# The decayed scores of a chunked recurrence: levels of 32 and 64 tokens as full 128 by 128 products with masks

## The chip, the core and the metric

The program runs on one core of one Trainium2 chip. Five engines work side by side, each through its own queue in the order of the program: TensorE (PE, with its weight loads shown apart as PEld), VectorE (DVE), ScalarE (ACT), GpSimd (POOL) and SyncE (SP, which issues the loads of weights). The metric is the device time of one execution in microseconds (us).

## What is computed

Two blocks of a language model run over 256 tokens of width 1024, in float32. The first block has two layers, and each has a mixer with a gated recurrence over 8 heads. That recurrence is what the change touches. It goes in chunks of 64 tokens, `gc` is the logarithm of the forget gate, and a state is carried from chunk to chunk:

```python
def step(state, inp):
    qc, kc, vc, gc = inp
    cum = jnp.cumsum(gc, axis=2)
    diff = cum[:, :, :, None, :] - cum[:, :, None, :, :]
    decay = jnp.where(causal, jnp.exp(jnp.where(causal, diff, 0.0)), 0.0)
    scores = jnp.einsum('bhtk,bhtsk,bhsk->bhts', qc, decay, kc)
    o = (jnp.einsum('bhts,bhsv->bhtv', scores, vc)
         + jnp.einsum('bhtk,bhkv->bhtv', qc * jnp.exp(cum), state))
...
```

Around it stand nine projections of the 256 tokens (values, forget gate, queries, a short convolution's three inputs, three gates), three output projections and a feed-forward; then come the mixture of experts and the second block. None of that is changed.

## The kernel before

Weights are streamed: SP loads pieces of 128 by 1024, ACT rounds each to a high part (`wh`, line 139), DVE subtracts to get the low part (`wl`, line 141), and PE does three products for each pair of tiles (lines 207 to 209: high by high, high by low, low by high). This is the main stream, written by `mixer` for the recurrence's part of the program. Six pieces of each part are held, so the splits run ahead of PE until that ring is full. A projection of 256 columns takes two pieces and 48 main products of 128 by 256.

The recurrence, `hgrn`, is a side generator. After half a projection and again after a projection, the main stream steps it twice (`tick`), at a lower priority; from these priorities a scheduler fixes each engine's order when the kernel is built. `hgrn` takes the eight heads in two halves of four, so the two layers together have four halves. A half computes the scores of every pair (s, t) in a tile of 128 tokens by levels. A first level (`md`) covers pairs within a block of 8. Then, for a block size m of 8, 16, 32, 64 and 128, the pairs with s in the left and t in the right half of a block of 2m are done: `e` holds keys decayed to the left half's end and queries decayed from there, and a product of `e` with itself gives their scores. For each level there are two steps of ACT and DVE work (lines 735 to 746) before its products.

What happens at each level before the change, for each of the two token tiles and four heads of a half:

- m = 8: one full 128 by 128 product per head into a PSUM bank, all four heads in one bank; then `put` copies the valid pairs to `Sc` by a mask on DVE (`copy_predicated`, line 724).
- m = 16: the same full products into a bank `hold` for each token tile, which is kept.
- m = 32: for each head two products of 32 by 32, written into corners of the bank of m = 16, over what stood there (lines 763 to 769).
- m = 64: for each head one product of 64 by 64, likewise; then one `put` per bank moves the levels 16, 32 and 64 together, by the mask `m16`.
- m = 128: one full product per head across the two token tiles.

All of these products go through `mm` (line 203); in the trace a float32 product stands as two matmul records with two weight loads. The side work has three PSUM banks (`sd`), of which `hold` keeps two from m = 16 to m = 64. At the end of a half, once the output gate `sg` is there, the scores meet the values, a norm is taken, and PE transposes the result (line 805), after which the last output projection but one can read it.

Of the kernel before, what the change touches and what calls it, by code (L numbers as in the profile page):

```python
# [16 lines left out]
P = 128  # L17
D = 1024
S = 256
NT = S // P  # L20
# [3 lines left out]
NE = 8  # L24
EPS = 1e-6
BIG = 1.0e30
# [21 lines left out]
class Kernel:  # L48
# [48 lines left out]
    # raws: what one DMA loads; pieces: what is split at a time into two parts of 12 bits each  # L97
# [11 lines left out]
    def pump(self, limit=1 << 30):  # L109
        nc = self.nc  # L110
        while True:
# [3 lines left out]
            i = self.dma_i  # L115
# [13 lines left out]
            if i < len(self.pieces) and i < self.freed + SPLIT_BUFS and self.pieces[i][0] < self.dma_i:  # L129
# [5 lines left out]
                with self.tc.high_priority(offset=SPLIT_SOONER):  # L135
                    # small operations where a phase's chain runs beside them
                    m = n // (FINE_BY if i in self.fine else 1)
                    for c in range(0, n, m):
                        nc.scalar.copy(hi[:, c:c + m], raw[:, c:c + m])  # L139
                        with self.tc.issue_after(self.hold) if self.hold is not None else nullcontext():  # L140
                            nc.vector.tensor_sub(lo[:, c:c + m], raw[:, c:c + m], hi[:, c:c + m].bitcast(F32))  # L141
# [10 lines left out]
    # while arenas are free, raws of the next phase go there  # L152
# [24 lines left out]
    # steps: how many of its steps follow each unit of the main stream  # L177
# [19 lines left out]
    def urgent(self):  # L197
        # no sooner than the last branch
        return self.tc.high_priority(offset=min(CHAIN_SOONER, self.tc.tile_snap_priority() - self.floor))

# [17 lines left out]
    def rsqrt_mean(self, ss, n):  # L218
        """(ss / n + eps) ** -0.5; overwrites ss"""
# [5 lines left out]
    def mean_sq(self, halves, c=1.0):  # L225
        """(c * c * mean of squares + c * c * eps) ** -0.5 over two halves of 512; c a power of two.
        halves: yields each half when it is there"""
# [19 lines left out]
    def prenorm(self, t, gt, out=None):  # L247
        """x[t] -> normalised tokens [128, 1024]"""
# [12 lines left out]
    def put_hT(self, t, xs):  # L261
        """transpose normalised tokens into hT hi/lo"""
# [15 lines left out]
    # boundary: post(t) puts the phase's output for token tile t into x  # L278
# [7 lines left out]
    # the second token tile's transposes come after the first tile's products  # L286
# [6 lines left out]
    def down(self, key, lhs, nk, post, to_next):  # L293
        """tokens-stationary product with K = nk*128, 1024 columns.
        post(t, banks): adds to x.  to_next: (prenorm, after T0 matmuls ...)"""
# [38 lines left out]
    def norm_next(self, gt):  # L334
        """steps to go from x to hT of the next phase, used by down()"""
# [18 lines left out]
    def norm_post(self, pg, scale):  # L354
        """x += scale * rmsnorm(product) * pg"""
# [12 lines left out]
    # weights-stationary projection: out [128, 2, 256]  # L368
# [20 lines left out]
    # tokens-stationary projection: out [128 tok, n, 256]  # L389
# [21 lines left out]
    def ffn(self, n, post, to_next):  # L411
# [4 lines left out]
        def finish_g(g, gt):  # L416
            """gt: [128 tok] x T tiles of G columns"""
# [63 lines left out]
    def consts(self):  # L481
        nc = self.nc
        g = nc.gpsimd
        # small per-channel parameters: rows in, columns out
# [26 lines left out]
        # lower bounds: cumulated softmax over the two layers, less its first  # L511
# [19 lines left out]
        # masks over [s, t]  # L531
# [4 lines left out]
        v16 = lambda t: t.rearrange("p (n i) -> p n i", i=16)  # L536
        self.m16 = self.cst("m16", [P, P])      # t in a later block of 16 than s
        g.memset(self.m16, 1.0)
        sel(v16(self.m16), [[16, 8], [0, 16]], -1, -1)
        self.m8 = self.cst("m8", [P, P])        # same block of 16, t in its second half, s in its first  # L540
        g.memset(self.m8, 1.0)
        sel(v16(self.m8), [[16, 8], [0, 16]], 15, -1)
        sel(v8(self.m8), [[8, 16], [0, 8]], -1, -1)
        self.md = self.cst("md", [P, P])        # same block of 8, s <= t
# [30 lines left out]
    def mixer(self, l, post, to_next):  # L575
# [13 lines left out]
        # forget gate  # L589
# [20 lines left out]
        # short convolution of b * u, gated by c  # L610
# [71 lines left out]
    def hgrn(self, l, V, LF, Kt, Qt, box):  # L682
        """decayed scores by halving: for block sizes m the pairs (s in a left half, t in the
        right half) are referred to the left half's end, so no exponent is above 0; inside
        blocks of 8 the middle is the reference and exponents stay within 8 * ln(1e-6) / 2"""
        nc = self.nc
        mul, sub, add = nc.vector.tensor_mul, nc.vector.tensor_sub, nc.vector.tensor_add
        # scores are kept 2**-20 smaller, so that no product overflows outside the blocks either
# [5 lines left out]
        for h in range(2):  # L694
# [38 lines left out]
            hold = None  # L733
            for m in (8, 16, 32, 64, 128):
# [13 lines left out]
                if m == 8:  # L748
                    for t in range(NT):
# [4 lines left out]
                        put(t, pt, self.m8)  # L754
                        yield
                elif m == 16:
                    hold = [self.sd_ps((P, 4, P)) for _ in range(NT)]
                    for t in range(NT):
                        for j in range(4):
                            c = slice(j * S + t * P, j * S + (t + 1) * P)  # L760
                            self.mm(hold[t][:, j, :], e[:, c], e[:, c], True, True)
                    yield
                elif m in (32, 64):
                    for t in range(NT):
                        for j in range(4):
                            for b in range(0, P, 2 * m):
                                c = j * S + t * P + b
                                self.mm(hold[t][b:b + m, j, b + m:b + 2 * m], e[:, c:c + m],
                                        e[:, c + m:c + 2 * m], True, True)
                    if m == 64:  # L770
                        for t in range(NT):
                            put(t, hold[t], self.m16)
                    yield
# [7 lines left out]
            # values, norm over a head's values, output gate  # L781
# [58 lines left out]
    def moe_consts(self):  # L840
# [6 lines left out]
        self.tri = t[:, 2, :]                   # s < t  # L847
# [6 lines left out]
        self.jlt = t[:, 4, 0:NE * NE].rearrange("p (e j) -> p e j", j=NE)  # j < e  # L854
# [7 lines left out]
        # the norm's gain goes with the features, its factor with the tokens  # L862
        nc.vector.tensor_mul(self.rw, self.rw, bc(self.moe_g.unsqueeze(2), [P, KD, NE]))

    def moe_enter(self):
        """from x to tokens in two parts, and each token's place with its experts; the norm's
        factor does not change the order of the logits and is put to the experts' products"""
# [39 lines left out]
    def route(self, t, pl):  # L907
        """the two experts of each token"""
# [3 lines left out]
        # rank of each expert: greater logits, or equal ones at a lower index, come first  # L912
# [10 lines left out]
    def places(self):  # L923
        """place of each token in its expert's list, and the places' one-hot"""
# [12 lines left out]
    def gates(self):  # L937
        """softmax over the chosen two; the largest count of an expert's tokens"""
# [20 lines left out]
    def moe_places(self):  # L959
        """one-hot with the places on the partitions"""  # L960
# [9 lines left out]
    def gather(self, q):  # L970
        """the tokens of experts 2q, 2q + 1, features on the partitions"""
# [19 lines left out]
    def slots_r(self, ohs, out):  # L991
        """the norm's factor of the token at each place"""
# [96 lines left out]
    def final_norm(self, nxt):  # L1089
        """x[t] = rmsnorm(x[t]) * fin, and the next phase's norm of that"""  # L1090
# [5 lines left out]
        def after(t):  # L1096
# [13 lines left out]
            # mean square of w * r without a further pass  # L1110
# [18 lines left out]
    def moe_rest(self):  # L1129
        """experts with more than 128 tokens: their places 128..255"""  # L1130
# [99 lines left out]
    def consts2(self):  # L1230
        """relative bias, causal masks, window counts, head masks"""
        nc, g, I = self.nc, self.nc.gpsimd, self.ins
        c = self.arena(7, (P, 16, P))
        self.R = c[:, 0:8, :].rearrange("p (h a) b -> p h (a b)", h=4)       # bias of (t, s), t in the second tile
        self.invc = c[:, 8, 0:16]
        self.cpen = c[:, 12, :]                 # 0 where s <= t, else -BIG  [t, s]
# [3 lines left out]
        self.ki4 = c[:, 13, :]                  # row c to rows 32 h + c  # L1240
# [4 lines left out]
        self.hm = c[:, 14, 0:8]                 # four 32-row heads, two 64-row heads  # L1245
# [7 lines left out]
        # 1 / (t + 1)  # L1253
        g.iota(self.invc, pattern=[[1, 16]], base=1, channel_multiplier=0, allow_small_or_imprecise_dtypes=True)
        nc.vector.reciprocal(self.invc, self.invc)
        # bias by distance, then one row per t through DRAM
# [4 lines left out]
        n1 = 255                                # rv[j] = bias of distance max(255 - j, 0)  # L1261
# [7 lines left out]
        # row t reads rv[127 - t : 127 - t + 256]; loaded with t reversed, turned by a permutation  # L1269
# [25 lines left out]
    def mix2_params(self, l):  # L1295
        """tiles and parameters of the mixing; their arenas are free once the feed-forward before is
        past its first 8 row blocks of w_down"""
# [27 lines left out]
    def mix2(self, l, post, to_next):  # L1325
# [9 lines left out]
        # token-layout values of gmlp and attention  # L1335
# [8 lines left out]
        # index queries, keys and weights  # L1344
# [423 lines left out]
```

## Time and profile before

| | us |
|---|---|
| three runs | 2904.30, 2908.52, 2911.13 |
| their median | 2908.52 |
| span of the profiled execution | 2903.8 |
| PE busy in it | 2846.2 |
| PEld busy | 2575.5 |
| DVE busy | 2023.8 |
| ACT busy | 1643.3 |
| POOL busy | 84.6 |

The span runs from the first to the last instruction of the program in the profiled execution; the timed runs include what lies around it. PE's records overlap, since products are pipelined, so a busy PE can still be a slow one: what a product costs is read from the distance between the starts of neighbours in the timeline, not from its record's length. The granted clock of a stretch is 1.00 at 2.4 GHz and 0.50 at 1.2 GHz.

### The profile page before, as it was taken

The page shows a single profiled execution, that of the slowest core. Times are in us where ns is not written, and L with a number is a line of the kernel's source. Part 1 is how long each engine was busy: PE and PEld are TensorE (multiplying, and loading weights), DVE is VectorE, ACT ScalarE, POOL GpSimd, SP SyncE. Part 2 cuts the span into 40 slices and gives each one's busy share as a digit, 9 for nine tenths or more (in the row PEclk, how much of TensorE's full clock was granted, in tenths as well). Part 3 has the DMA queues.
Part 4 walks back from the last instruction along what each step waited for, and adds up shares of the span by engine and source line. Part 5 has one row for each costly group of instructions (what it writes and reads, how often), then busy time and mean ns, then how long its engine had stood idle before and what let it go on. Part 6 is the DMA issues. An engine that isn't in the chain of part 4 may idle for free. (4 is left out here: it accounts for less than half of the span.)

```text
span 2903.8 us, 47599 instructions
## 1 busy us (share of the span) xinstructions
PE 2846.2 (98%) x18752; PEld 2575.5 (89%) x18752; DVE 2023.8 (70%) x2631; ACT 1643.3 (57%) x2188; POOL 84.6 (3%) x161
## 2 busy tenths in 40 slices
PE   8999999999999999999999989999999999999999
PEld 8998999999898887877877779899999899899997
DVE  5665655576659888888888865579765555697654
ACT  6543544564447776777777754466554444565543
POOL 1000000000000000000000010100000001000000
PEclk9998999999999999999999989999999999999999
DMA  7453565555456999999999965654655556546553
GB/s 248 145 175 102 177 192 186 186 160 158 155 190 223 331 333 350 338 341 353 329 345 359 346 209 185 198 170 135 204 189 186 187 186 200 168 137 199 183 182 109
DMA packets 425047, 635.00 MB, mean 219 GB/s; under 512 B 20186, under 2 KB 298896, under 8 KB 424816
## 3 DMA queue, kind: packets, MB, share of 16 engines
q1 hardware_dynamic: 421184, 621.65, 65.1%
q0 software_dynamic: 3632, 10.24, 1.3%
q8 instruction: 148, 2.42, 0.4%
q14 instruction: 83, 0.68, 0.1%
HBM read 630.76 MB, written 1.05 MB: 218 GB/s over the span
## 5 line engine op out<-in xcount | busy, mean ns | idle before, releaser
L141 DVE TENSOR_TENSOR wl<-wr,wh 128x1024 fp32r<-128x1024 f32 (+2 forms) x1265 | 1408.9, 1139 | 605.4 <-ACT wh L139 596.4
L139 ACT CAST wh<-wr 128x1024 fp32r<-128x1024 f32 (+2 forms) x1265 | 1201.0, 983 | 709.9 <-PE mm L208 360.9
L207 PE MATMUL mm<-hhi,wh 128*128 128x256 f32 x3360 | 961.8, 286 | 0.0
L208 PE MATMUL mm<-hlo,wh 128*128 128x256 f32 x3360 | 959.7, 286 | 0.0
L209 PE MATMUL mm<-hhi,wl 128*128 128x256 f32 x3360 | 958.7, 285 | 0.0
L207 PEld LDWEIGHTS mm<-hhi,wh 128*128 128x128 f32 x3360 | 646.1, 192 | 3.2 <-issue 2.0
L208 PEld LDWEIGHTS mm<-hlo,wh 128*128 128x128 f32 x3360 | 646.3, 192 | 1.9 <-issue 0.7
L209 PEld LDWEIGHTS mm<-hhi,wl 128*128 128x128 f32 x3360 | 646.2, 192 | 1.4 <-issue 0.3
L208 PE MATMUL mm<-wl,a 128*128 128x512 f32 (+1 forms) x1336 | 514.1, 385 | 2.2
L207 PE MATMUL mm<-wh,a 128*128 128x512 f32 (+1 forms) x1336 | 509.9, 382 | 0.0
L209 PE MATMUL mm<-wh,a 128*128 128x512 f32 (+1 forms) x1336 | 508.3, 380 | 0.0
L208 PEld LDWEIGHTS mm<-wl,a 128*128 128x128 f32 x1336 | 251.3, 188 | 65.9 <-DVE wl L141 17.5
L207 PEld LDWEIGHTS mm<-wh,a 128*128 128x128 f32 x1336 | 251.4, 188 | 49.6 <-issue 1.5
L209 PEld LDWEIGHTS mm<-wh,a 128*128 128x128 f32 x1336 | 251.5, 188 | 45.5
L208 PE MATMUL sd<-wl,a 128*128 128x512 f32 x352 | 145.2, 412 | 1.1
L209 PE MATMUL sd<-wh,a 128*128 128x512 f32 x352 | 140.1, 398 | 3.7 <-PEq L1132 3.7
L207 PE MATMUL sd<-wh,a 128*128 128x512 f32 x352 | 117.4, 399 | 0.0
L207 PE MATMUL mm<-a,wh 128*128 128x256 f32 x384 | 113.8, 296 | 0.0
L208 PE MATMUL mm<-a,wh 128*128 128x256 f32 x384 | 113.0, 294 | 0.0
L209 PE MATMUL mm<-a,wl 128*128 128x256 f32 x384 | 112.7, 294 | 0.0
L212 ACT CAST a<-t 128x256 fp32r<-128x256 f32 (+1 forms) x114 | 49.3, 432 | 108.9 <-DVE t L453 105.8
L209 PE MATMUL mm<-wh,hlo 128*128 128x256 f32 x352 | 104.5, 297 | 2.8 <-DVE hlo L213 2.8
(323 smaller groups left out, 2528.7 us busy)
## 6 DMA issues: line engine op xcount, KB each, us to landing
wr<-in_expert_w_dram SPq DMA_DIRECT2D x515, 512.0 KB, 5.4
wr<-in_w_in_dram SPq DMA_DIRECT2D x240, 512.0 KB, 3.9
wr<-in_ffn_w_gu_dram SPq DMA_DIRECT2D x176, 512.0 KB, 3.5
wr<-in_ffn_w_down_dram SPq DMA_DIRECT2D x88, 512.0 KB, 3.4
wr<-in_dense_w_dram SPq DMA_DIRECT2D x66, 512.0 KB, 3.6
wr<-in_w_out_dram SPq DMA_DIRECT2D x32, 512.0 KB, 4.1
wr<-in_w_proj_conv_dram SPq DMA_DIRECT2D x16, 512.0 KB, 4.5
wr<-in_w_proj_hgrn_dram SPq DMA_DIRECT2D x16, 512.0 KB, 4.5
```

The source lines that it names most:

```text
L139: nc.scalar.copy(hi[:, c:c + m], raw[:, c:c + m])
L141: nc.vector.tensor_sub(lo[:, c:c + m], raw[:, c:c + m], hi[:, c:c + m].bitcast(F32))
L207: mm(out, l[0], r[0], start=start, stop=False)
L208: mm(out, l[0], r[1], start=False, stop=False)
L209: mm(out, l[1], r[0], start=False, stop=stop)
L212: self.nc.scalar.copy(hi, src)
```

## The change

Levels 8, 16, 32 and 64 all do the same full product of `e` with itself per head and token tile, into a bank of their own that is freed at once. What a full product yields outside the level's own pairs is wrong, and later levels overwrite it: the mask of a level takes every pair in which t lies in a later block of m than s, and the greater levels come after. For m = 64 the valid part is one rectangle, so ACT copies it without a mask. `hold` is gone. Levels 16, 32 and 64 each have a step per token tile now, so a half has three steps more. The masks are `m8`, `m16` and `m32` by one rule; one `affine_select` fewer is done at the start. All other lines of the diff are comments.

```diff
-        self.m16 = self.cst("m16", [P, P])      # t in a later block of 16 than s
-        g.memset(self.m16, 1.0)
-        sel(v16(self.m16), [[16, 8], [0, 16]], -1, -1)
-        self.m8 = self.cst("m8", [P, P])        # same block of 16, t in its second half, s in its first
...
+        self.later_block = {}
+        for m in (8, 16, 32):
+            t = self.later_block[m] = self.cst(f"m{m}", [P, P])
+            g.memset(t, 1.0)
+            sel(t.rearrange("p (n i) -> p n i", i=m), [[m, P // m], [0, m]], -1, -1)
...
-            hold = None
             for m in (8, 16, 32, 64, 128):
...
-                if m == 8:
+                if m < 128:
                     for t in range(NT):
                         pt = self.sd_ps((P, 4, P))
                         for j in range(4):
                             c = slice(j * S + t * P, j * S + (t + 1) * P)
                             self.mm(pt[:, j, :], e[:, c], e[:, c], True, True)
-                        put(t, pt, self.m8)
+                        if m == 64:
+                            nc.scalar.copy(Sc[0:64, 2 * t, :, 64:P], pt[0:64, :, 64:P])
+                        else:
+                            put(t, pt, self.later_block[m])
                         yield
-                elif m == 16:
-                    hold = [self.sd_ps((P, 4, P)) for _ in range(NT)]
-                    for t in range(NT):
-                        for j in range(4):
-                            c = slice(j * S + t * P, j * S + (t + 1) * P)
-                            self.mm(hold[t][:, j, :], e[:, c], e[:, c], True, True)
-                    yield
-                elif m in (32, 64):
-                    for t in range(NT):
-                        for j in range(4):
-                            for b in range(0, P, 2 * m):
-                                c = j * S + t * P + b
-                                self.mm(hold[t][b:b + m, j, b + m:b + 2 * m], e[:, c:c + m],
-                                        e[:, c + m:c + 2 * m], True, True)
-                    if m == 64:
-                        for t in range(NT):
-                            put(t, hold[t], self.m16)
-                    yield
```

PE, level of 32 tokens of the first half in the first layer. Before (`sd_` is a score bank, `t_` is `e`, `mm_` the main stream's bank):

```order
L203 MATMUL sd_1266<-t_169_1276 32x32
L207 MATMUL mm_1419<-hhi_145,wh_1209 128x256
L203 MATMUL sd_1266<-t_169_1276 32x32
L208 MATMUL mm_1419<-hlo_146,wh_1209 128x256
L203 MATMUL sd_1266<-t_169_1276 32x32
L209 MATMUL mm_1419<-hhi_145,wl_1210 128x256
L203 MATMUL sd_1266<-t_169_1276 32x32
L207 MATMUL mm_1419<-hhi_145,wh_1227 128x256
L203 MATMUL sd_1266<-t_169_1276 32x32
```

and in the changed kernel:

```order
L203 MATMUL sd_1349<-t_175_1317 128x128
L207 MATMUL mm_1405<-hhi_145,wh_1211 128x256
L203 MATMUL sd_1355<-t_175_1317 128x128
L203 MATMUL sd_1349<-t_175_1317 128x128
L208 MATMUL mm_1405<-hlo_146,wh_1211 128x256
L203 MATMUL sd_1355<-t_175_1317 128x128
L203 MATMUL sd_1349<-t_175_1317 128x128
L209 MATMUL mm_1405<-hhi_145,wl_1212 128x256
L203 MATMUL sd_1355<-t_175_1317 128x128
L203 MATMUL sd_1349<-t_175_1317 128x128
L203 MATMUL sd_1355<-t_175_1317 128x128
```

Of the sixteen narrow products, each of which had a main product behind it, none is left; eight full ones stand there, with three main products among them.

DVE, in the same half at the level of 64 tokens. Before (line 724 is `put`, 141 a weight split, 622 and 634 the convolution's work, 713 the next half's first step):

```order
L713 TENSOR_TENSOR t_298_2325<-a_41_184 128x1024
L141 TENSOR_TENSOR wl_1465<-wr_1150,wh_1464 128x1024
L622 TENSOR_TENSOR a_135_1000<-a_135_1000,mm_1419 128x2x256
L141 TENSOR_TENSOR wl_1483<-wr_1213,wh_1482 128x1024
L724 COPY_PREDICATED Sc_1029<-m_333,sd_1266 128x512
L724 COPY_PREDICATED Sc_1029<-m_333,sd_1267 128x512
```

and in the changed kernel (lines 722, 141, 620 and 632 are the same in its numbering; 741 is the last part of `e` for m = 128):

```order
L741 TENSOR_TENSOR t_195_1479<-t_195_1479,a_42_185 128x4x128
L632 SCALAR_TENSOR_TENSOR t_220_1678<-a_135_1002,cols,t_220_1678 128x256 x2
L722 COPY_PREDICATED Sc_1031<-m_339,sd_1349 128x512
L141 TENSOR_TENSOR wl_1455<-wr_1152,wh_1454 128x1024
L722 COPY_PREDICATED Sc_1031<-m_339,sd_1355 128x512
L620 TENSOR_TENSOR a_135_1002<-a_135_1002,mm_1405 128x2x256
```

Before, one pair of puts (`m_333` is `m16` there) closed the levels 16 to 64; now the levels 16 and 32 have a pair each (`m_339` is the mask of 32 tokens), with a weight split between its two.

## Rows read from the trace of the kernel before

**Rows 1.** The page's part 1, busy time by engine, and its clock line
```profile
PE 2846.2 (98%) x18752; PEld 2575.5 (89%) x18752; DVE 2023.8 (70%) x2631; ACT 1643.3 (57%) x2188; POOL 84.6 (3%) x161
...
PEclk9998999999999999999999989999999999999999
```

**Rows 2.** The page's part 4, the chain that ended last
```profile
PE 39%; DVE 2%; issue 1%; POOL 1%; ACT 0%; POOLq 0%; DVEq 0%; ACTq 0%
```

**Rows 3.** Waits of PE, in total, times, longest
```profile
PE sd L268 <- DVE t L254: 18.9, 13, 12.3
PE sd L805 <- DVE t L801: 9.2, 8, 2.3
PE sd L268 <- DVE t L1120: 8.6, 2, 6.5
```

**Rows 4.** Timeline of PE in a full level: start, us, line, tiles, count
```profile
118.22 0.38 PE L203 MATMUL sd<-t 128*128 128x128 f32 x2
118.36 0.37 PE L207 MATMUL mm<-hhi,wh 128*128 128x256 f32 x1
118.56 0.38 PE L203 MATMUL sd<-t 128*128 128x128 f32 x2
118.70 0.37 PE L208 MATMUL mm<-hlo,wh 128*128 128x256 f32 x1
...
120.51 0.38 PE L203 MATMUL sd<-t 128*128 128x128 f32 x2
120.65 0.36 PE L207 MATMUL mm<-hhi,wh 128*128 128x256 f32 x1
120.85 0.28 PE L208 MATMUL mm<-hlo,wh 128*128 128x256 f32 x1
120.97 0.28 PE L209 MATMUL mm<-hhi,wl 128*128 128x256 f32 x1
```

**Rows 5.** The same in a level of 32 tokens
```profile
123.46 0.25 PE L203 MATMUL sd<-t 128*32 128x32 f32 x2
123.64 0.39 PE L208 MATMUL mm<-hlo,wh 128*128 128x256 f32 x1
123.95 0.25 PE L203 MATMUL sd<-t 128*32 128x32 f32 x2
124.13 0.38 PE L209 MATMUL mm<-hhi,wl 128*128 128x256 f32 x1
124.44 0.25 PE L203 MATMUL sd<-t 128*32 128x32 f32 x2
```

**Rows 6.** The same in a level of 64 tokens
```profile
138.05 0.33 PE L203 MATMUL sd<-t 128*64 128x64 f32 x2
138.31 0.39 PE L208 MATMUL mm<-hlo,wh 128*128 128x256 f32 x1
138.63 0.33 PE L203 MATMUL sd<-t 128*64 128x64 f32 x2
138.88 0.38 PE L209 MATMUL mm<-hhi,wl 128*128 128x256 f32 x1
139.20 0.27 PE L203 MATMUL sd<-t 128*64 128x64 f32 x1
```

**Rows 7.** Four stretches: busy us (count) by engine, granted clock, DMA share, GB/s
```profile
core 0: us, PE busy (x) PEld busy (x) DVE busy (x) ACT busy (x) POOL busy (x), PEclk, DMA share, GB/s
122.97:143.89 20.92, 20.92 (x121) 16.40 (x121) 11.26 (x20) 4.63 (x6) 0.00 (x0) 0.84 0.30 98
248.22:272.52 24.30, 24.30 (x122) 18.32 (x122) 7.74 (x9) 5.02 (x5) 0.00 (x0) 0.65 0.19 64
643.91:666.04 22.13, 22.13 (x121) 17.11 (x121) 11.26 (x20) 4.63 (x6) 0.00 (x0) 0.77 0.29 93
769.69:789.97 20.28, 20.28 (x122) 15.55 (x121) 7.76 (x9) 5.04 (x5) 0.00 (x0) 0.83 0.38 127
```

**Rows 8.** The first of these stretches, line 203 alone: PE, PEld, clock
```profile
122.97:143.89 20.92, 6.81 (x48) 3.97 (x49) 0.84 0.30 98
```

**Rows 9.** Timeline of PE in a stretch at half clock
```profile
133.19 0.41 PE L209 MATMUL mm<-hhi,wl 128*128 128x256 f32 x1
133.40 0.41 PE L207 MATMUL mm<-hhi,wh 128*128 128x256 f32 x1
```

**Rows 10.** Weight loads of score products by shape: busy us, mean ns
```profile
L203 PEld LDWEIGHTS sd<-t 128*128 128x128 f32 x160 | 23.7, 191 | 0.0
L203 PEld LDWEIGHTS sd<-t 128*32 128x32 f32 x128 | 9.5, 119 | 10.1 <-issue 4.9
L203 PEld LDWEIGHTS sd<-t 128*64 128x64 f32 x64 | 7.0, 155 | 5.0 <-issue 2.0
```

**Rows 11.** The recurrence's first half in the first layer, busy us by engine
```profile
103.17:169.30 66.13, 66.13 (x503) 61.48 (x502) 51.26 (x76) 28.36 (x34) 0.00 (x0) 0.95 0.43 136
```

**Rows 12.** Groups of DVE, and of ACT, from 100 to 170 us: busy, mean ns, idle
```profile
L724 DVE COPY_PREDICATED Sc<-m,sd 128x512 f32<-128x512 int32 x4 | 2.9, 737 | 2.4 <-PE sd L203 2.4
L779 ACT COPY Sc<-sd 128x512 f32<-128x512 f32 x1 | 0.6, 578 | 0.0
```

**Rows 13.** Who waited for whom, in the whole span: total us, times, longest
```profile
DVE Sc L724 <- PE sd L203: 29.1, 14, 3.7
```

More of the change, by code (lines that the diff above doesn't have):

```diff
@@ L416, in finish_g @@
         def finish_g(g, gt):
+            pass
         gts = []
@@ L535, in consts @@
         v8 = lambda t: t.rearrange("p (n i) -> p n i", i=8)
-        v16 = lambda t: t.rearrange("p (n i) -> p n i", i=16)
-        self.m16 = self.cst("m16", [P, P])
-        g.memset(self.m16, 1.0)
-        sel(v16(self.m16), [[16, 8], [0, 16]], -1, -1)
-        self.m8 = self.cst("m8", [P, P])
-        g.memset(self.m8, 1.0)
-        sel(v16(self.m8), [[16, 8], [0, 16]], 15, -1)
-        sel(v8(self.m8), [[8, 16], [0, 8]], -1, -1)
+        self.later_block = {}
[3 more added lines that the diff above has]
+            sel(t.rearrange("p (n i) -> p n i", i=m), [[m, P // m], [0, m]], -1, -1)
         self.md = self.cst("md", [P, P])
```

## The prediction

> **What bounds the kernel now.** I read the page first: PE is busy for 2846.2 us of the 2903.8, 98%, and its clock line shows 9 nearly everywhere [rows 1]. The chain that ended last goes through PE far more than through any other engine [rows 2]. PE's own waits are few: 18.9 and 8.6 us at the norms between phases, and 9.2 us at the transposes that end a half of the recurrence (line 805) [rows 3]. So in both mixers the main stream sets the time, the recurrence's products are pushed in between its products, and each us of PE that they take is a us of the whole, as long as the weights are split in time. The question is what a product costs there; for that I went to PE's timeline and read distances between starts.
>
> Main products of 128 by 256 start 0.12 us apart when nothing stands between them (the last two rows of [rows 4]). In a full level (m = 16 in the first half) eight score products and seven main ones take 120.85 - 118.22 = 2.63 us; less 7 x 0.12 = 0.84 that leaves 1.79 us, **0.224 us for a full product** [rows 4]. In the level of 32 tokens one narrow product and one main product take 0.49 us (123.46 to 123.95 to 124.44), so the **narrow product costs 0.37 us** [rows 5], more than a full one. In the level of 64 tokens the pair takes 0.575 us (138.05 to 138.63 to 139.20), so that **product costs 0.455 us**, twice a full one [rows 6]. The reader sees why in the same rows: behind a narrow product the next product starts only when the narrow one is nearly at its end, and the other way round, while among full ones starts lie well within the neighbour's record.
>
> There is a second loss. I laid a window from the first narrow product to the first product of level 128 over each of the four halves: 20.92, 24.30, 22.13 and 20.28 us, at granted clocks of 0.84, 0.65, 0.77 and 0.83 [rows 7]. So in each of them the clock falls from 2.4 to 1.2 GHz for a part. Before the falls PE was alternating narrow and main products. At half clock main products start 0.21 us apart instead of 0.12 [rows 9].
>
> **The change part by part.** What goes: per half 16 products of 32 by 32 and 8 of 64 by 64. Each window of [rows 7] holds 48 matmul records of line 203, two to each of these 24 products [rows 8], and 121 PE records in all with the one that straddles its start, so 120 - 48 = 72 main products, 72 x 0.12 = 8.64 us. (The windows with 122 hold one more that straddles.) What the windows take beyond that is 12.28, 15.66, 13.49 and 11.64 us, together 53.07 us. Of this 16 x 0.37 + 8 x 0.455 = 9.56 us per half, 38.2 in all, are the products at full clock; the other 14.8 us are the half clock, which strikes the main products too.
>
> What comes: per half 16 full products, 64 in all. The trace shows the same operation, `e` with itself into a bank, at level 8 and 16, between the same main products, at 0.224 us and with main products 0.12 us apart, which is the full clock [rows 4]: 64 x 0.224 = 14.3 us. The changed order puts them among main products in the same way, so I take the same price.
>
> Sum on PE: 53.1 - 14.3 = **38.8 us less**. No part of it lies beside other work that then sets the end: in these windows DVE is busy for only 11.26 of 20.92 us and 7.74 of 24.30 [rows 7], it is PE that others wait for.
>
> What moves to DVE: two puts more per half, eight in all, at 0.737 us [rows 12], 5.9 us. The cover is PE's main stream. In the first half of the first layer DVE is busy for 51.26 of 66.13 us [rows 11]. After the change this stretch should take 66.13 - 12.28 + 16 x 0.224 = 57.4 us, and DVE's work 51.26 + 2 x 0.737 = 52.7 us: 92%, still under PE. In the densest part (from the puts of level 16 on) DVE can fall some us behind, but in the changed order a low part is first read no earlier than 111 main products after the product that the put ahead of it waits for, the least distance there was before as well; that is 111 x 0.12 = 13.3 us of room. I take nothing for it. If the cover went, the 5.9 us would be paid in full.
>
> What moves to ACT: two copies per half of a quarter of a bank. The trace has none of this size; a whole bank took 0.578 us [rows 12], so it is between nothing and 0.58 us each, 4.6 us in all at most, on an engine that is busy for 28.36 of 66.13 us [rows 11]. Nothing for the end.
>
> The three steps more per half move the end of each layer's second half back by 24 main products. It then still lies over 80 main products, about 10 us, ahead of the projection that reads it; behind the last transposes come one DVE operation and one split, so this is free. One mask operation fewer on POOL at the start, and banks that come free sooner: nothing waits there.
>
> What stays and may change in size: the eight waits at line 805, 9.2 us, the longest 2.3 [rows 3]. DVE's order around them shifts. If all went, 9.2 us would be gained; if all were as long as the longest, 8 x 2.3 - 9.2 = 9.2 us would be lost. I take none of it and keep both ends.
>
> The sum against the profiled execution: 2903.8 - 38.8 = 2865.0 us. The median is 4.7 us above that span, the runs lie from 2904.3 to 2911.1; I leave these 4.7 us as they are: **2908.5 - 38.8 = 2869.7 us**, a gain of 1.3%.
>
> **Weighing a rule.** The rows show that a narrow product costs more than a full one, 0.37 and 0.455 against 0.224 us [rows 4 to 6]. The Trainium skill says otherwise of narrow shapes: "TensorE: Matmul & The Clock Gate", has the cost of a product follow its moving columns down to a floor of some 25 ns (section "Back-to-back issue gap"), and has a weight load take about 0.83 ns per column (section "LDWEIGHTS (loading the stationary operand)"). By that page, as an estimate with two loads to a product, the three shapes would cost 0.053, 0.107 and 0.213 us; the narrow ones would be 6.8 us in all, the full ones 13.6, and the change would lose 6.8 us. The full product agrees with the page, the narrow ones are four to seven times above it, and the measurement decides. Neither section speaks of shapes that alternate on PE, as they do here all the time.
>
> **Rivals.**
> (a) *Cost by width.* If the narrow products were cheap and the stretches long for another reason, full products would cost PE time. By weight loads, 119 and 155 against 191 ns [rows 10], a narrow one would be 0.224 x 119 / 191 = 0.14 and 0.18 us, the four halves 64 x 0.14 + 32 x 0.18 = 14.7 us against 14.3: no change, 2908 us. By bare width (a quarter, a half) they would be 64 x 0.056 + 32 x 0.112 = 7.2 us: 7.1 us lost, 2916 us. This is also where the page above leads. Against it: the long distances sit exactly at the narrow products and end with them, and no engine is late there.
> (b) *The clock falls all the same.* If the half clock came from something else in this place, only the 38.2 - 14.3 = 23.9 us at full clock are won: 2884.6 us. For it: at 133.2 us main products follow one another, no narrow one stands between them, and the clock is still at half [rows 9]. Against it: the level of 16 just ahead runs in the same mixture of work with main products 0.12 us apart [rows 4], at full clock.
> (c) *DVE's queue takes PE's place, and the kernel gets slower.* A put waits for its products, and weight splits are queued behind it; PE then waits for a low part. DVE has waited at puts 14 times for 29.1 us, the longest 3.7 [rows 13]. Reckoned on the first half, with eight puts: DVE's 52.7 us and these waits must exceed 57.4 + 13.3 = 70.7 us before PE waits at all, which is 2.25 us at each put; and by 9.7 us more, 3.5 us at each, before the gain of 38.8 us is gone. At the longest wait at each, 52.7 + 29.6 - 70.7 = 11.6 us would be lost in each half: 2908.5 - 38.8 + 46 = 2916 us. Against it: over all 24 puts of today that is 1.2 us each, about half of what it takes to begin, and among PE's waits in the mixers there is none for a low part [rows 3].
> (d) *The edit changes nothing of the pattern*, because the scheduler puts it otherwise: excluded, the changed order has no narrow product left in it.
>
> **How the numbers follow.** Forecast 2869.7 us: 0.82. Rival (b), 2885: 0.07. Rival (c) in a mild form that gives back 5 to 15 us, 2875 to 2885: 0.04; in full, 2916: 0.02. Rival (a): 0.05, half of it without change and half slower. The range takes the forecast with the ends of the waits at line 805, 2860.5 to 2879, and reaches on to rival (b) with about 2 us for the spread of runs: 2861 to 2887. Rival (a) and the full (c) stay out, 0.07. Within 0.2% (5.8 us), about what a measurement of this kernel can tell from no change, lies half of (a), 0.03; slower the other half and the full (c), 0.04; faster 0.93.
>
> **What would show it.** Right: no narrow form among the products of line 203; eight full products at 1.8 us in levels 32 and 64 as well; a clock of 1.0 through all four halves; a window from the first product of level 32 to level 128 that is 8 to 12 us shorter; waits of PE little changed. Wrong: idle time of PE ahead of lines 207 to 209 released by line 141 (rival c), a clock below 1 in the halves (rival b), or full products further apart than 0.224 us in the new levels (rival a).

## The result, and the profile after

The changed kernel takes 2868.45 us (median of four runs, 2867.16 to 2869.08); the kernel before, run again beside it, 2909.8 us (2904.30 to 2911.13). The ratio is 0.9862, 95% interval 0.985 to 0.9873: **faster by 1.4%**, 1.3 us from the forecast of 2869.7 us.

The page's part 1 and its clock line, after; the lines of before are in [rows 1]:

```profile
PE 2804.7 (98%) x18688; PEld 2554.8 (89%) x18688; DVE 2026.4 (71%) x2639; ACT 1645.4 (57%) x2196; POOL 86.3 (3%) x162
...
PEclk9999999999999999999999989999999999999999
```

PE is busy for 41.5 us less at the same share, with 64 records fewer; DVE has eight operations more and 2.6 us. POOL has one operation more: the changed start sets four masks in place of three and has five `affine_select` as before, not one fewer as the section on the change has it; at 1.7 us of POOL this moves nothing here. The fourth digit of the clock line, where the first layer's recurrence stands, has risen from 8 to 9.

Timeline of PE in the level of 32 tokens of the first half, after (start us, us, line, tiles, count); [rows 5] is the same place before:

```profile
126.66 0.38 PE L203 MATMUL sd<-t 128*128 128x128 f32 x2
126.79 0.37 PE L207 MATMUL mm<-hhi,wh 128*128 128x256 f32 x1
127.00 0.61 PE L203 MATMUL sd<-t 128*128 128x128 f32 x4
...
128.71 0.36 PE L207 MATMUL mm<-hhi,wh 128*128 128x256 f32 x1
128.91 0.28 PE L208 MATMUL mm<-hlo,wh 128*128 128x256 f32 x1
```

There is no narrow form left. Eight products and four main ones take 128.91 - 126.66 = 2.25 us; less 4 x 0.12 that is 1.77 us, 0.22 us for each, as in the full level of [rows 4].

The four windows from the first product of level 32 to that of level 128, after (columns as in [rows 7]):

```profile
core 0: us, PE busy (x) PEld busy (x) DVE busy (x) ACT busy (x) POOL busy (x), PEclk, DMA share, GB/s
126.66:141.71 15.05, 15.05 (x131) 15.05 (x129) 14.97 (x26) 7.28 (x9) 0.00 (x0) 1.00 0.44 140
240.17:255.11 14.94, 14.94 (x131) 14.94 (x129) 10.35 (x13) 6.84 (x9) 0.00 (x0) 1.00 0.51 158
626.49:641.54 15.05, 15.05 (x130) 15.05 (x129) 14.98 (x26) 7.28 (x9) 0.00 (x0) 1.00 0.45 139
739.97:754.91 14.94, 14.94 (x130) 14.94 (x129) 10.36 (x13) 6.83 (x9) 0.00 (x0) 1.00 0.66 215
sum 59.98, PE 59.98 PEld 59.98 DVE 50.66 ACT 28.22 POOL 0.00; mean PE 14.99 PEld 14.99 DVE 12.67 ACT 7.05 POOL 0.00
```

Each window now holds 96 main products in place of 72, since two more steps of the half lie in it, and 16 full score products. 59.98 us less 4 x 96 x 0.12 = 46.08 leaves 13.9 us for the score products, against 53.07 in [rows 7]: 39.2 us less. The clock stands at 1.00 in all four, and PEld is busy from end to end, where it was busy for 16.40 of 20.92 us.

Waits of PE in the whole span, and that of DVE at the puts (total us, times, longest); before: [rows 3, 13], with the branch there in the last row here:

```profile
PE sd L268 <- DVE t L254: 19.1, 13, 12.5
PE sd L788 <- DVE t L784: 10.1, 8, 2.3
PE sd L268 <- DVE t L1103: 8.7, 2, 6.5
PE sd L209 <- PEq L1115: 5.5, 1, 5.5
...
DVE Sc L722 <- PE sd L203: 15.2, 8, 3.7
```
```profile
PE sd L209 <- PEq L1132: 3.7, 1, 3.7
```

The waits of PE are as they were, within 1 us each (line 788 is 805 of before), except at the branch in the mixture of experts (line 1115, 1132 before), which had 3.7 us and now has 5.5. DVE waits less at the puts than before, 15.2 for 29.1 us, though there are eight more of them.

### The profile page after: what moved, and what is told of

Its sections match the earlier page's. It is cut to its first block, busy times and chain, and to the rows that moved or that the text cites. A ratio compares the mean times of both kernels' runs of the same rounds, so it can differ in the third digit from the quotient of the medians.

```text
span 2866.1 us, 47497 instructions
## 1 busy us (share of the span) xinstructions
PE 2804.7 (98%) x18688; PEld 2554.8 (89%) x18688; DVE 2026.4 (71%) x2639; ACT 1645.4 (57%) x2196; POOL 86.3 (3%) x162
## 5 line engine op out<-in xcount | busy, mean ns | idle before, releaser
L207 PE MATMUL mm<-a,wh 128*128 128x256 f32 x384 | 110.6, 288 | 0.0
L208 PE MATMUL mm<-a,wh 128*128 128x256 f32 x384 | 109.1, 284 | 0.0
```

The lines of the kernel that those rows point to most:

```text
L207: mm(out, l[0], r[0], start=start, stop=False)
L208: mm(out, l[0], r[1], start=False, stop=False)
```

## The experiments

The theory is that a narrow product was dear because PE has to change between its shape and the full one each time that it goes from a main product to a narrow one and back (a visit, below), and that such stretches brought the clock down. Against it stood: that narrowness itself is dear whatever stands beside it; that narrow products cost by their width; that the corners of a shared bank are dear; that DVE's queue is about to set the time. All kernels but one start from the changed kernel, 2868.45 us.

**Level 64 narrow again, in a bank of its own.**

```diff
...
-                            self.mm(pt[:, j, :], e[:, c], e[:, c], True, True)
+                            c0 = j * S + t * P
+                            if m in (64,):
+                                for b in range(0, P, 2 * m):
+                                    self.mm(pt[b:b + m, j, b + m:b + 2 * m], e[:, c0 + b:c0 + b + m],
+                                            e[:, c0 + b + m:c0 + b + 2 * m], True, True)
+                            else:
+                                self.mm(pt[:, j, :], e[:, c], e[:, c], True, True)
...
```

> The changed kernel (2868.5 us) with the products of level 64 alone narrow again, 64 by 64, in a bank of their own and copied in the same way. Theory A (a narrow product is dear because PE changes between its shape and the full one at each visit, that is at each run of narrow products between main ones): a visit costs 0.455 us for its first product, 0.15 for each further one. Second halves have 8 visits of one product, +1.85 us each; first halves 4 visits with 8 products, +0.6 each: +4.9 us, 2873. Theory B (narrowness itself is dear, whatever stands beside it): 0.455 us for each product in all halves, +7.4 us, 2876. Rival W (cost by width): no loss, 2867 to 2868. Rival H (what was dear was writing into the corners of a bank that holds an earlier level): no loss, 2868. The clock may stay up in all cases.

2871.19 us (2870.49 to 2873.29): 2.7 us more than the changed kernel. Windows over such a level, of a first half (4 visits, 8 products, 4 main products) and of half a level of a second half (4 visits, 4 products):

```profile
134.21:136.87 2.66, 2.66 (x22) 2.00 (x21) 1.39 (x5) 1.23 (x2) 0.00 (x0) 1.00 0.61 190
248.15:250.35 2.20, 2.20 (x13) 1.55 (x13) 0.00 (x0) 0.95 (x1) 0.00 (x0) 1.00 0.78 238
```

Less 4 x 0.12, that is 1.72 us for four lone products, 0.43 each, and 2.18 us for eight in four visits: a further product in a visit costs (2.18 - 1.72) / 4 = 0.115 us. That is theory A's pattern, and a bank of its own has not made them cheap. The total is under A's 4.9 us and would not tell A from its rivals; the windows do. By their prices the level costs 2.18 us in a first half and 8 x 0.43 = 3.44 us in a second, against 1.77 us with full products, 4.2 us more over the four halves; the profiled executions lie 3.6 us apart (2869.7 and 2866.1).

**Level 32 narrow again, in a bank of its own** (the same edit for m = 32 with its two products of 32 by 32 per head, and ACT copying the two corners).

> The changed kernel (2868.5 us) with the products of level 32 alone narrow again, 32 by 32, in a bank of their own. Theory A (change of shape at each visit): 0.37 us for the first product of a visit, 0.12 for each further one; second halves have 16 visits of one, +4.1 us each, first halves 8 visits with 16 products, +2.1 each: +12.5 us at full clock, and falls of the clock at least in the second halves (up to 15 us in the kernel before): 2881 to 2890. Theory B (narrowness itself): +4.1 us in all four halves, +16.5 us, and falls in all four: 2885 to 2900. Rivals W (cost by width) and H (corners of a used bank): 2868 to 2870, no fall of the clock.

2881.46 us (2879.06 to 2884.74), 13.0 more. PE's timeline in the first half, and windows over 8 visits each: the first half's level (16 products), then the two parts of a second half's (8 products each):

```profile
126.61 0.25 PE L203 MATMUL sd<-t 128*32 128x32 f32 x2
126.79 0.38 PE L207 MATMUL mm<-hhi,wh 128*128 128x256 f32 x1
127.11 0.26 PE L203 MATMUL sd<-t 128*32 128x32 f32 x4
127.29 0.39 PE L208 MATMUL mm<-hlo,wh 128*128 128x256 f32 x1
127.61 0.26 PE L203 MATMUL sd<-t 128*32 128x32 f32 x4
```
```profile
core 0: us, PE busy (x) PEld busy (x) DVE busy (x) ACT busy (x) POOL busy (x), PEclk, DMA share, GB/s
126.61:130.80 4.19, 4.19 (x41) 2.96 (x41) 3.06 (x6) 1.81 (x4) 0.00 (x0) 1.00 0.37 119
241.68:245.72 4.04, 4.04 (x26) 2.79 (x26) 2.56 (x3) 1.94 (x4) 0.00 (x0) 0.94 0.35 113
249.01:253.33 4.32, 4.32 (x26) 2.95 (x25) 2.40 (x3) 0.53 (x3) 0.00 (x0) 0.85 0.35 121
```

In these rows a visit of one or of two products takes the same 0.50 us with its main product (126.61 to 127.11 to 127.61). Eight main products taken off (0.96 us), 16 products in 8 visits cost 3.23 us and 8 products in 8 visits 3.08 and 3.36. Twice the products at about the same price: it is mainly the visits that are paid. The last two windows show clocks of 0.94 and 0.85, so a part of their price is half clock; the next experiment has such a window at full clock.

**Both levels narrow, in banks of their own.**

> Both levels, 32 and 64, narrow again, each in a bank of its own, so that only the shapes of the kernel before come back and not its shared bank. In the second halves narrow products stand singly between main ones, in the first halves often two or three together. Theory A: per half 9.56 us for narrow products at full clock in the second halves, about 6.3 in the first, against 3.58 in the changed kernel: +17 us and the half clock in the second halves: about 2890 to 2897. Theory B: 9.56 us in all halves, +24 us and the half clock everywhere as before: 2900 to 2908. Rivals W and H: 2868.

2887.56 us in one run, 19 more than the changed kernel and 22 less than the kernel before, which has the same narrow products. A first half's level 32, and a part of a second half's at full clock:

```profile
126.52:130.71 4.19, 4.19 (x42) 2.96 (x42) 3.06 (x6) 1.82 (x4) 0.00 (x0) 1.00 0.37 119
249.36:253.22 3.86, 3.86 (x25) 2.63 (x25) 2.69 (x3) 0.67 (x2) 0.00 (x0) 1.00 0.42 136
```

A lone product costs (3.86 - 0.96) / 8 = 0.36 us, and 16 products in 8 visits (4.19 - 0.96) = 3.23, so a further one costs 0.04 us, less than the 0.12 that I gave it, and the clock fell for less time (mean 0.99 from 100 to 800 us, 0.97 in the kernel before); so the time is below A's range. Theory B, 2900 to 2908, has fallen: the shapes are the old ones, and what differs is how they stand among the main products.

With these prices the sum for level 32 alone closes too. Two first halves cost 3.23 - 1.77 us more than full products and two second halves 16 x 0.36 - 1.77 us, together 10.9 us. In that profiled execution the clock fell twice in each second half, each time for 3.41 us; the first of the four:

```profile
245.21:248.62 3.41, 3.41 (x17) 3.35 (x18) 0.95 (x2) 2.48 (x5) 0.00 (x0) 0.50 0.48 154
```

A main product takes 0.21 us at half clock for 0.12 at full, so by estimate such a stretch costs 3.41 x (1 - 0.12 / 0.21) = 1.46 us, and four of them 5.8 us. That makes 16.7 us, and the spans lie 16.7 us apart (2882.8 and 2866.1); the medians lie 13.0 apart, as the other three runs were shorter.

**Both levels narrow, put together by a priority.**

```diff
...
+                        with self.urgent() if m in (32, 64) else nullcontext():
+                            for j in range(4):
...
```

`urgent` raises the priority of what is written under it, so that the scheduler puts these products ahead of the main ones that wait.

> Both levels narrow as in the kernel with 32 and 64 narrow, but with a priority that puts them together: visits of 8 or 16 products of 32 by 32 and of 4 or 8 of 64 by 64, with no main product between. Theory A (each visit pays once): per half about 4 visits, 2 x (0.37 + 7 x 0.12) + 2 x (0.455 + 3 x 0.15) = 4.2 us against 3.58: +2.5 us, 2871, and no fall of the clock. Theory B (narrowness itself): 9.56 us per half, +24 us, 2892, and more where the clock falls.

2863.06 us (2861.79 to 2863.45): 24.5 us less than the same products strewn among main ones, and even 5.4 us less than the changed kernel. PE in the first layer's second half:

```profile
235.70 1.01 PE L203 MATMUL sd<-t 128*128 128x128 f32 x34
236.64 0.39 PE L207 MATMUL mm<-a,wh 128*128 128x256 f32 x1
```

The first row is one full product and 16 of 32 by 32: 0.94 us to the next main product, 0.72 without the full one, 0.045 us for each narrow product. Theory A holds; its own estimate, 2871, was too high because I had set the further products too dear.

**The kernel before, with that priority alone.**

```diff
...
+                    with self.urgent():
+                        for t in range(NT):
...
```

> The kernel before (2909.3 us) with one edit: its narrow products, still in the corners of the shared bank, get the priority that puts them together (visits of 8 products of 32 by 32 and 4 or 8 of 64 by 64). Nothing else of the change is in it: no masks, no bank of its own, no full product. Theory A (each visit between products of full shape pays about 0.33 us, a further narrow product 0.03 to 0.12 us): per half 3 or 4 visits and 24 products, about 2.7 us instead of 9.56, and no half clock (14.8 us in all): 2909 - 27 - 15 = 2867, between 2862 and 2872. If the gain of the change came from the masks, the own banks or the freed PSUM: no gain here, 2905 to 2910.

2862.57 us (2861.01 to 2865.58) against 2909.47 beside it: ratio 0.9843, interval 0.9827 to 0.986. One line, with the shared bank, the corners and the mask `m16` all in place, gives what the whole change gives, and 5.9 us more. About 1.9 of these 5.9 us stand at the branch in the mixture of experts, where PE waits 5.5 us in the changed kernel and 3.6 here (3.6 too in the experiment before). PE in the first half, the wait at the branch, and a window over all four halves' scores with its clock:

```profile
120.58 1.79 PE L203 MATMUL sd<-t 128*128 128x128 f32 x28
122.30 0.39 PE L207 MATMUL mm<-hhi,wh 128*128 128x256 f32 x1
```
```profile
PE sd L209 <- PEq L1133: 3.6, 1, 3.6
```
```profile
100.00:760.00 660.00, 650.89 (x5231) 631.77 (x5231) 430.22 (x558) 337.32 (x428) 15.03 (x18) 1.00 0.58 174
```

The row of 28 records is two full products, eight of 32 by 32 and four of 64 by 64, and takes 1.72 us to the next main product. So neither masks nor banks made the gain.

**Which side of the product is it?** Narrow stationary side, all 128 moving columns:

```diff
...
+                                    self.mm(pt[b:b + m, j, :], e[:, c0 + b:c0 + b + m],
+                                            e[:, c], True, True)
...
```

> The changed kernel (2868.5 us) with levels 32 and 64 as 16 products of 32 stationary columns and 8 of 64, each against all 128 moving columns, into rows of a bank of their own; placed among main products as in the kernel with both levels narrow (2887.6 us). If the dear thing is the change of the stationary's width: the visits pay as there, 2887 to 2895. If it is the shortness of the moving side: 24 products at no more than 0.224 us, 5.4 instead of 3.58 us per half, 2876 or less.

and its mirror image, all 128 stationary columns, narrow moving side:

```diff
...
+                                    self.mm(pt[:, j, b + m:b + 2 * m], e[:, c],
+                                            e[:, c0 + b + m:c0 + b + 2 * m], True, True)
...
```

> The mirror image: levels 32 and 64 as 16 products of all 128 stationary columns against 32 moving ones and 8 against 64, placed in the same way. If the dear thing is the stationary's width: no visit pays, 24 products bound by their weight loads at up to 0.224 us, +7 us at most, 2872 to 2876, clock up. If it is the shortness of the moving side: 2887 or more.

The first takes 2896.23 us, 1.2 us above the range, since a visit of it is dearer than I had put it (below); the second 2872.79, inside its range; one run each. PE in a second half's level 32 of the first, with the window over eight visits:

```profile
245.29 0.41 PE L203 MATMUL sd<-t 128*32 128x128 f32 x2
245.62 0.38 PE L207 MATMUL mm<-a,wh 128*128 128x256 f32 x1
245.94 0.41 PE L203 MATMUL sd<-t 128*32 128x128 f32 x2
```
```profile
245.29:250.42 5.13, 5.13 (x25) 2.63 (x25) 3.23 (x4) 2.43 (x4) 0.00 (x0) 1.00 0.34 107
```

and of the second:

```profile
239.49 0.30 PE L203 MATMUL sd<-t 128*128 128x32 f32 x2
239.63 0.37 PE L207 MATMUL mm<-a,wh 128*128 128x256 f32 x1
239.84 0.30 PE L203 MATMUL sd<-t 128*128 128x32 f32 x2
...
240.18 0.30 PE L203 MATMUL sd<-t 128*128 128x32 f32 x2
```

With a narrow stationary side the pair takes 0.65 us, 0.53 for the product, and PEld is busy for only 2.63 of 5.13 us. With a narrow moving side the pair takes 0.345 us (239.49 to 239.84 to 240.18), 0.225 for the product, the same as with 128 moving columns. So it is the stationary side's width. The reader sees the mechanism in the starts: beside a product of the same width the next one starts while the last is still on its way, and weight loads fill PE's time (15.05 of 15.05 us in the windows of after); at a change of width the next main product starts 0.33 us after a narrow one and that at 0.32 us after a main one, near the end of each record. The Trainium skill, "TensorEngine Tiling (Array Packing)", section "Tiling Modes", says that changing the tiling mode, and not only the tile, drains the engine; these rows agree in when the next product starts. They put the price of going and coming back at about 0.32 us (0.36 for a lone product of 32 by 32, less 0.04 for a further one; 0.43 less 0.115 for 64 by 64).

**Levels 32 and 64 packed.** e is laid out with both token tiles' left halves side by side and the right halves behind them, so that one full product per head does both tiles:

```diff
...
+                    for j in range(4):
+                        self.mm(pt[:, j, :], e[:, j * S:j * S + P], e[:, j * S + P:(j + 1) * S], True, True)
+                    yield
+                    for i in range(P // m):
+                        t, b = i * 2 * m // P, i * 2 * m % P
+                        nc.scalar.copy(Sc[b:b + m, 2 * t, :, b + m:b + 2 * m],
+                                       pt[i * m:(i + 1) * m, :, i * m:(i + 1) * m])
...
```

> The changed kernel with levels 32 and 64 packed: the left halves of both token tiles stand side by side in e, the right halves behind them, so that one full product per head does a level for both tiles, and ACT copies the valid squares (four of 32, two of 64) to their places. 8 full products per half instead of 16, 4 puts fewer on DVE, 6 copies on ACT instead of 2. Theory A: PE pays 0.224 us per full product, 32 fewer: -7.2 us, 2861. If PE were no longer what sets the time in these stretches: 2868. If ACT's small copies hold the weight splits: above 2869.

2860.18 us (2855.55 to 2860.44), ratio to the kernel before 0.9828, interval 0.9811 to 0.9844: 8.3 us under the changed kernel, the lowest median of the versions that do the whole work. The wait at the branch is 3.8 us here, 1.7 of the 8.3. Half the full products of these levels are gone, at the same price for each. The same window as above, of the first half:

```profile
127.76:141.06 13.30, 13.30 (x115) 13.30 (x114) 13.30 (x23) 8.30 (x13) 0.00 (x0) 1.00 0.52 158
```

13.30 - 96 x 0.12 = 1.78 us for eight products. DVE is busy through the whole of it, and so is PE; that the room ahead of the low parts is the reason fits the prediction, but no run here shows it.

**Is DVE near its limit?** Each put of levels 8, 16 and 32 done three times.

```diff
-                            put(t, pt, self.later_block[m])
+                            for _ in range(3):
+                                put(t, pt, self.later_block[m])
```

> The changed kernel (2868.5 us) with each put of levels 8, 16 and 32 done three times over: 12 masked copies more per half on DVE, 12 x 0.62 to 0.74 = 7.4 to 8.8 us per half, 30 to 35 us of DVE work in all, none on PE. If PE's stream covers DVE (the prediction's reading, with 13.3 us of room between a put's wait and the low parts behind it): within 3 us of the changed kernel, 2868 to 2872. If DVE's queue was about to set the time (the prediction's rival c): up to 35 us more, 2885 to 2903.

2866.75 us (2865.77 to 2867.77): no loss. The group of these puts from 100 to 170 us, here and in the changed kernel:

```profile
L722 DVE COPY_PREDICATED Sc<-m,sd 128x512 f32<-128x512 int32 x18 | 11.9, 733 | 0.1
L722 DVE COPY_PREDICATED Sc<-m,sd 128x512 f32<-128x512 int32 x6 | 4.4, 740 | 0.4 <-PE sd L203 0.4
```

So the cover of PE's main stream is real, with room for 7.5 us more of DVE work in this half, by estimate 30 us over the four. Rival (c) needed 18 us more than DVE's work in a half, as waits of 2.25 us at each of the eight puts, 72 us in all; DVE waited at the puts for 15.2 us in the changed kernel. It was far away.

**Levels 32 and 64 left out.**

This version leaves out their products, puts and copies; `e` is still computed.

> The changed kernel without the products, puts and copies of levels 32 and 64; e is still computed, the scores of these levels are left out. If each full product costs 0.224 us on the path: 64 x 0.224 = 14.3 us less, 2854. If part of it lay under other work: less than that, 2855 to 2868.

2855.02 us in one run, span 2853.3: 12.8 us off the span instead of 14.3. In this run the second layer had a stretch at half clock that the changed kernel had not, 0.84 us behind a wait of PE for the transposes of a half. Its window, and that wait in the changed kernel, which is as long and has full clock behind it:

```profile
758.85:762.26 3.41, 3.41 (x18) 3.41 (x17) 2.26 (x4) 1.04 (x1) 0.00 (x0) 0.50 0.45 154
```
```profile
772.01 0.66 PE L788 MATMUL sd<-ident,t 128*128 128x128 f32 x4 [2.26 <-DVE t L784]
```
```profile
772.01:782.01 10.00, 10.00 (x84) 10.00 (x85) 5.55 (x6) 4.63 (x5) 0.00 (x0) 1.00 0.48 144
```

By the estimate above 3.41 us at half clock cost 1.5 us; with it the sum is met. So in this one run the products of these levels lie on the path in full.

## Why the prediction was right

- *What sets the time*: PE's main stream. Right: taking the full products out, or halving them, moved the end by about their own price, and 30 us of DVE work cost nothing.
- *Price of a product*: 0.37 and 0.455 us for a narrow one among main ones, 0.224 for a full one. The full ones measured 0.22 in the new levels; lone narrow ones measured 0.36 and 0.43 again, in banks of their own. As a reading of that place the prices were right. As prices of a shape they would have been wrong: together, the products of 32 by 32 cost 0.045 us. The prediction spoke of shapes that alternate, but had not thought of keeping the shapes and ending the alternation.
- *Sum*: forecast 38.8 us less, measured 39.2 in the four windows. The span is 37.7 us shorter; the wait at the branch took 1.8 us back. The medians lie 41.4 us apart; the profiled run of after took 2868.2 us, 2.1 over its span, so a span of 2903.8 belongs to a run of about 2906, on the short side of the runs before. So the span gained 1.1 us less than forecast and the medians 2.6 us more; that the total came within 1.3 us is in part luck, as the prediction took the 4.7 us between its span and its median over unchanged.
- *Sign of the windows*: they were to be 8 to 12 us shorter and are 5.3 to 9.4 ([rows 7] less the windows of after). The sign had left out the 24 main products, 2.88 us, that each window now holds more; without main products the four are 8.75, 12.24, 9.96 and 8.22 us shorter.
- *Half clock*: 14.8 us were put down to it. The clock is at 1.00 in all windows of after, and of these 14.8 us nothing has come back. That the narrow visits brought it down is shown as far as the falls are gone with them, by the priority alone too (1.00 in its window from 100 to 760 us). What in them does it is open. Where eight visits, seventeen main products and eight visits follow one another (the second halves with level 32 narrow), the clock still falls, to 0.94 and 0.85 in the windows above; with as many visits, each longer, against 128 moving columns it stays at 1.00. So the number of visits alone does not decide it; no run here tells what does. Rival (b), that the clock falls all the same in these levels, is out. One fall in the second layer is another matter and stands in no term of the prediction, the one at PE's wait for the transposes:

```profile
808.38:811.79 3.41, 3.41 (x18) 3.41 (x18) 3.41 (x4) 2.49 (x3) 0.00 (x0) 0.50 0.31 105
```

  The kernel before had it, and so had five of the ten other versions, the two with the priority and the one with the levels left out among them; the changed kernel did not, with the same wait. By the estimate of 1.5 us it is a small part of the span's gain that is not the products' doing; why it comes and goes is open.
- *DVE*: forecast 52.7 of 57.4 us in the first half, measured (the window from the first score product to the end of the convolution, after):

```profile
104.08:161.36 57.28, 57.28 (x487) 57.28 (x486) 51.79 (x78) 28.68 (x36) 0.00 (x0) 1.00 0.51 156
```

51.79 of 57.28 us.
- *Waits at line 805*: taken as unchanged, 9.2 us; measured 10.1. *Mask operations on POOL*: one fewer was reckoned, one more is there; nothing was put down for it.
- *Rival (a)*, cost by width, found its counterpart: within a visit, and only there, products do cost by width, 0.04 us for 32 and 0.115 for 64 columns. The prediction's estimate from the Trainium skill, "TensorE: Matmul & The Clock Gate", section "LDWEIGHTS (loading the stationary operand)", 0.053 and 0.107 us, is near that state; it is four to seven times too low where the width changes at each step.

## What to carry to other kernels

Before replacing small products by large ones, look at what stands between them: if products of another stationary width alternate with the main stream, give them a priority that puts them together, which here gave 47 us for one line. Where they can't be put together, a full product with a mask (0.22 us) is cheaper than a visit for one narrow product (0.36 to 0.43), and packing two half-empty products into one full one is better still. Read prices from the distance of starts in the place itself; a price so read holds for the neighbourhood, not for the shape.

## What was not expected of the hardware

- A float32 product with 128 stationary columns, among main products, costs the same 0.22 us for 32 and 128 moving columns, with weight loads back to back in the windows of after. The Trainium skill, "TensorE: Matmul & The Clock Gate", section "LDWEIGHTS (loading the stationary operand)", has a load take as many ns as it has columns, divided by 1.2, whatever the contraction: 107 ns for 128; twice that is, as an estimate, 0.21 us. The trace agrees.
- Sixteen products of 32 by 32 in a row cost 0.045 us each with the change of width in the price, each of them two matmul records with two weight loads. A further one in a visit costs about 0.04 us in short visits; in that long one it is (0.72 - 0.36) / 15 = 0.024 us.
- A visit of 32 stationary columns costs 0.53 us with 128 moving columns against 0.36 with 32, though with full stationary width the moving columns made no difference.
